# A hybrid attention and recurrence block on one Trainium2 core: the query norms move ahead of the turn, the causal mask moves into a matrix product

## The chip, the core and the metric

One core of a Trainium2 chip runs the whole program: TensorE (PE in the profile; its weight loads are PEld), VectorE (DVE), ScalarE (ACT), GpSimd (POOL), and SyncE (SP), which issues nearly all DMA transfers. Each engine has its own queue of instructions and works through it in order; semaphores hold one engine until another has produced what it reads. PSUM is the memory that TensorE's products add up in, SBUF the other one on the chip. The metric is device time of one execution in microseconds (us), the median of several.

## The reference, cut to what matters

```python
mod = silu(c) @ ada_w + ada_b                    # 2048 x 12288, one vector
h = rms_norm(x, norm_mix_g) * (1 + sc1) + sh1    # x: 256 x 2048
z = h @ w_in                                     # q, kc, vc, ks, vs, kw, vw, gl, xr, xg
q = rope(rms_norm(q, q_norm_g), pos)             # 8 heads of 128
ks = rope(rms_norm(ks, k_norm_g[1]), pos)        # 2 key heads; kw the same
gates = sigmoid(gl + gate_b)
o_attn = nsa_attention(...)   # gates of compressed, selected and window attention
o_rnn = rglru_branch(xr, xg, ...)                # causal conv, gated linear recurrence
x = x + gt1 * (concat(rms_norm(o_attn), rms_norm(o_rnn)) @ w_out)
x = x + gt2 * peer_ffn(rms_norm(x, norm_ffn_g) * (1 + sc2) + sh2, ...)
```

In `nsa_attention` each of three branches is a softmax of scaled scores under a mask. The sequence has 256 tokens, so both the selected branch and the window branch are plain causal attention over all of it, with other keys and values. `rglru_branch` computes `a = exp(-8 r softplus(-lam))` and `b = sqrt(1 - a^2) * i * u` and scans `h = a h + b` over the tokens. The last part, the feed-forward of 16384 experts, takes about three quarters of the time, and the change does not touch it.

## The kernel before

Tokens stand in two tiles of 128 (`tb` 0 and 1). The large products are made in three float32r passes, for which each weight tile (`raw`, 1 MB, by SP's queue) is split by ACT into `wh` (L206) and by DVE into the rest `wl` (L207). The input projection is computed in pieces: `q0` (heads 0 to 3 of q) first, then the key blocks, then the blocks b0 to b3, of which b2 holds heads 4 to 7 of q (`q1`) and b0, b1, b3 the recurrence's inputs. `rest` adds a block's products to `part` tiles on DVE (L544).

`ev_q` takes four heads of q: ACT sums the squares, DVE turns them by the rotary tables into `zr_q` (L610 to L613), PE transposes `zr_q` into the PSUM tile `tp_q` (L623), and ACT copies that to `qT`. Beside it DVE forms the inverse norms in `rsqrt` (L404 to L410: three setup operations and three Newton rounds of three, each dependent on the one before) and puts them, times the softmax scale, into `rq` (L640). Keys are treated otherwise: `ev_kv` multiplies the norms into `zr_k` on ACT (L659) before the transposes.

`scores(sp, g, tb)` handles four heads of key group g and one token tile, for both causal branches at once. For each head PE makes two products into `sc` (L808); DVE multiplies by `rq` (L799, only for `tb` 1, the unmasked half) and by `rq` with the mask added (L800), both from PSUM into the SBUF tile `pt`; DVE takes the maxima of `pt` (L803); ACT takes the exponentials of `pt` in place and their sums (L792). `sc`, `tp_q`, `cps`, `ptt`, `rp` and other small products share one PSUM tag with three buffers. `outputs` divides, weighs by the gates and multiplies by the values (`ptt`, `po`); for the compressed branch it multiplies `cs` by `rq` (L831) and adds a mask (L833). `recurrence(gr)` handles two of the eight channel blocks: convolution `u` on DVE (L748), products `rp` on PE (L753), tanh and exp on ACT, and a chain of DVE operations (L760 to L774) that ends in the scans.

`compress` makes the compressed keys: 64 products `cps` (L698), then a norm. `gate_logits` makes `gl`, from a weight tile of 128x384 that is loaded, split, and multiplied in three passes.

What else runs beside: the modulation vector's product with `ada_w`. Part of it is done on PE (`adp`, L268), part on DVE: an `av` tile of 128x2048 is loaded by SP (L219) and multiplied and summed by one DVE instruction of 2.28 us (L228). `av` has two buffers, and the `part` tiles occupy them; one comes free when the last transposes of `part_391` (`tp_r`) are done, the other only when those of `part_392` are, after `gl`.

The order on every engine is fixed when the program is built. A string names what runs beside what:

```python
PROG = 'q0 b0@.2 e0,k0,k1,p0 b1@.4 e1,b2,e2 s0|s1|r0,c0,b3 c1,g0@.2 e3 o0|o1|r1@.3 r2 s3@.25 s2 l0@.25 o2|o3|r3,l1@.3'
```

`e2` is `ev_q` for q1, `s0` to `s3` are the calls of `scores` (g = n // 2, tb = n % 2), `c1` ends `compress`, `g0` is `gate_logits`, `l0` and `l1` make the second `xg` block. Streams joined by `|` advance in turn, one `yield` each; `@.2` feeds that many `av` products for each `yield`. A scheduler then orders the instructions by readiness and priority. So s0 and s1 (key group 0) form a first score stretch, some 243 to 261 us, and s3 and s2 a second one, some 302 to 324 us. Two recurrences, r0 and r1, run beside or just behind the first, r2 and r3 around the second. Then come the output norms (`nha`, `nta`), the output projection `y` (from 366.75 us), the second norm, and from 476.57 us the query products `wq` of the feed-forward.

Of the kernel before, what the change touches and what calls it, by code (L numbers as in the profile page):

```python
# [7 lines left out]
F32 = mybir.dt.float32  # L8
F32R = mybir.dt.float32r
U32 = mybir.dt.uint32  # L10
I32 = mybir.dt.int32
AF = mybir.ActivationFunctionType
OP = mybir.AluOpType
AX = mybir.AxisListType

P = 128
# [51 lines left out]
def kernel(  # L68
# [512 lines left out]
    kT = zp.tile([P, 2, NG, S], F32, name="kT")  # L581
    vv = zp.tile([P, NT, 2, NG, HD], F32, name="vv")
    gates = zp.tile([P, NT, 24], F32, name="gates")
    rq = zp.tile([P, NT, NH], F32, name="rq")
    kcT = zp.tile([P, 32], F32, name="kcT")
    vc = zp.tile([16, NG, HD], F32, name="vc")

    win = oT.rearrange("p h t -> p (h t)").rearrange("p (a l g n) -> p a l g n", a=2, l=32, g=2)
    ckT = xgT.rearrange("p h t -> p (h t)")[:, 0:4 * S].rearrange("p (a g t) -> p a g t", a=2, g=2)
    V.memset(win[:, :, :, :, NCMP:16], 0.0)  # L590
# [38 lines left out]
    def ev_q(j, pst):  # L629
        tab = table(0)  # L630
        s = tp1.tile([P, NT, 4], F32, tag="ssq", bufs=2, name=f"ssq{j}")
        z = []
        for tb in range(NT):
            z.append(zrow(tp1, f"q{j}{tb}"))
            sumsq(s[:, tb], pst[tb], 4, f"q{j}{tb}")
            rope(z[tb], pst[tb], 4, tab[:, tb, 0], tab[:, tb, 1], f"q{j}{tb}")
            yield
        tp = transpose4(z[0], f"q{j}0")
        r = rsqrt(tp1, s.rearrange("p b h -> p (b h)"), HD, 8, f"q{j}")
        V.tensor_scalar(rq[:, :, 4 * j:4 * j + 4], r.rearrange("p (b h) -> p b h", b=NT), SCALE, None, OP.mult)  # L640
        yield
        A.copy(qT[:, 4 * j:4 * j + 4, tbs[0]], tp.rearrange("p (h t) -> p h t", h=4))
        tp = transpose4(z[1], f"q{j}1")
        yield
        A.copy(qT[:, 4 * j:4 * j + 4, tbs[1]], tp.rearrange("p (h t) -> p h t", h=4))
# [90 lines left out]
    def recurrence(gr):  # L736
        n = RG
        if True:
            u = rn.tile([P, n, S], F32, tag="u", bufs=RNB, name=f"u{gr}")
            ta = rn.tile([P, n, S], F32, tag="ta", bufs=RNB, name=f"ta{gr}")  # L740
            ti = rn.tile([P, n, S], F32, tag="ti", bufs=RNB, name=f"ti{gr}")
            xr = xrT[:, n * gr:n * gr + n]
            for c_ in range(n):
                k = n * gr + c_
                A.activation(u[:, c_], xr[:, c_, 0:S], AF.Identity, scale=sm[:, S_CW + k:S_CW + k + 1],
                             bias=sm[:, S_CB + k:S_CB + k + 1])
                for o in range(1, 4):
                    V.scalar_tensor_tensor(out=u[:, c_], in0=xr[:, c_, o:o + S],  # L748
                                           scalar=sm[:, S_CW + 8 * o + k:S_CW + 8 * o + k + 1], in1=u[:, c_],
                                           op0=OP.mult, op1=OP.add)  # L750
                rp = ps_a(f"rp{gr}{c_}")
                for a in range(2):
                    T.matmul(rp[:, a * S:(a + 1) * S], lw[:, a, k], u[:, c_], start=True, stop=True)  # L753
                A.activation(ta[:, c_], rp[:, 0:S], AF.Tanh, scale=0.5, bias=hb[:, 0, k:k + 1])
                A.activation(ti[:, c_], rp[:, S:2 * S], AF.Tanh, scale=0.5, bias=hb[:, 1, k:k + 1])
                A.activation(xr[:, c_, 0:S], ta[:, c_], AF.Exp, scale=nsp[:, k:k + 1], bias=nsp[:, k:k + 1])
                A.activation(ta[:, c_], ta[:, c_], AF.Tanh, scale=spl[:, k:k + 1], bias=spl[:, k:k + 1])

            d = xr[:, :, 0:S]
            V.tensor_scalar(d, d, 0.5, 0.5, OP.mult, OP.add)  # L760
            V.scalar_tensor_tensor(out=u, in0=ti, scalar=1.0, in1=u, op0=OP.add, op1=OP.mult)
            yield
            V.scalar_tensor_tensor(out=ti, in0=ta, scalar=1.0, in1=d, op0=OP.add, op1=OP.mult)
            A.activation(ta, ta, AF.Sqrt)
            yield
            V.scalar_tensor_tensor(out=d, in0=ti, scalar=2.0, in1=d, op0=OP.subtract, op1=OP.mult)
            V.tensor_scalar(ti, d, -2.0, -1.0, OP.mult, OP.add)
            yield
            V.tensor_tensor(u, u, d, OP.mult)
            yield  # L770
            V.scalar_tensor_tensor(out=u, in0=ta, scalar=-1.0, in1=u, op0=OP.mult, op1=OP.mult)
            yield
            for i in range(n):
                V.tensor_tensor_scan(d[:, i], ti[:, i], u[:, i], 0.0, OP.mult, OP.add)  # L774
            yield
# [4 lines left out]
    def scores(sp, g, tb):  # L780

        n = (tb + 1) * P
        sums = sp.tile([P, 4, 2], F32, tag=f"sums{tb}", bufs=1, name=f"sums{tb}{g}")
        pts = [sp.tile([P, 2, n], F32, tag=f"pt{tb}", bufs=4, name=f"pt{tb}{g}{hh}") for hh in range(4)]
        m2 = sp.tile([P, 4, 2], F32, tag=f"m2{tb}", bufs=1, name=f"m2{tb}{g}")
        held[g, tb] = sums, pts
        scs = {}
        for i in range(6):
            if 0 <= i - 2:
                hh = i - 2  # L790
                for br in range(2):
                    A.activation(pts[hh][:, br], pts[hh][:, br], AF.Exp, bias=m2[:, hh, br:br + 1],  # L792
                                 accum_out=sums[:, hh, br:br + 1])
            if 0 <= i - 1 < 4:
                hh = i - 1
                s3 = scs.pop(hh)[:, 0:2 * n].rearrange("p (b n) -> p b n", b=2)
                r1 = rq[:, tb, 4 * g + hh:4 * g + hh + 1]
                if tb == 1:
                    V.tensor_scalar(pts[hh][:, :, 0:P], s3[:, :, 0:P], r1, None, OP.mult)  # L799
                V.scalar_tensor_tensor(  # L800
                    out=pts[hh][:, :, n - P:n], in0=s3[:, :, n - P:n], scalar=r1,
                    in1=caus.unsqueeze(1).to_broadcast([P, 2, P]), op0=OP.mult, op1=OP.add)
                V.tensor_reduce(m2[:, hh], pts[hh], AX.X, OP.max, negate=True)  # L803
            if i < 4:
                h = 4 * g + i
                scs[i] = ps_a(f"sc{tb}{h}")
                for br in range(2):
                    T.matmul(scs[i][:, br * n:(br + 1) * n], qT[:, h, tbs[tb]], kT[:, br, g, 0:n], start=True, stop=True)  # L808
            yield

    def outputs(sp, g, tb):
# [12 lines left out]
        for hh in range(4):  # L824
# [3 lines left out]
        cm = con[:, C_CMP + 16 * tb:C_CMP + 16 * tb + 16].unsqueeze(1).to_broadcast([P, 4, 16])  # L828
        va = con[:, C_VAL + 16 * tb:C_VAL + 16 * tb + 16].unsqueeze(1).to_broadcast([P, 4, 16])
        mx = sp.tile([P, 4], F32, tag="cmx", bufs=2, name=f"cmx{g}{tb}")  # L830
        V.tensor_tensor(pc, cps[:, 0:64].rearrange("p (h n) -> p h n", h=4),  # L831
                        rq[:, tb, hs].unsqueeze(2).to_broadcast([P, 4, 16]), OP.mult)
        V.tensor_tensor(pc, pc, cm, OP.add)  # L833
        V.tensor_reduce(mx, pc, AX.X, OP.max)
        V.tensor_tensor(pc, pc, mx.unsqueeze(2).to_broadcast([P, 4, 16]), OP.subtract)
        A.activation(pc, pc, AF.Exp)
# [581 lines left out]
```

## Time and profile before

| | |
|---|---|
| median of 3 runs | 2052.03 us (2051.98 to 2058.9) |
| profiled execution | 2056.6 us, span 2054.8 us |
| mean granted clock of TensorE | 0.983 of full |
| PE busy | 1979.6 us, 96% of the span |
| DVE busy | 1451.0 us, 71% |
| ACT busy | 1016.1 us, 49% |

The span runs from the first instruction to the last on the core; the execution's own time is 1.8 us longer. Busy shares are means over stages that differ: the stages that the change touches lie between about 205 and 366 us, and in them the DVE is as busy as PE.

### The profile page before, as it was taken

How to read it: one execution, taken by the hardware profiler on the slowest of the kernel's cores; microseconds unless marked ns; L12 is line 12 of the kernel's file. 1: busy time of each engine (PE TensorE's matmuls, PEld its weight loads, DVE VectorE, ACT ScalarE, POOL GpSimd, SP SyncE). 2: the span in 40 equal slices, each digit the busy share in tenths (PEclk: the TensorE clock that was granted, in tenths of full speed). 3: DMA queues.
4: the chain of work that ended last, by engine and by line, in shares of the span. 5: the costliest groups of instructions: out<-in, count | busy, mean ns of one | idle time of the engine just before them, and what ended most of it. 6: DMA issues, size and time to landing. Idle time of an engine off the chain costs nothing.

```text
span 2054.8 us, 31264 instructions
## 1 busy us (share of the span) xinstructions
PE 1979.6 (96%) x12602; PEld 1751.4 (85%) x12602; DVE 1451.0 (71%) x2149; ACT 1016.1 (49%) x1454; POOL 61.0 (3%) x95
## 2 busy tenths in 40 slices
PE   5999998998999999999999999999999999999998
PEld 4777565788999999998888789899999889999997
DVE  7888999887999666546667766665555555555566
ACT  2544676455446988645444334444444444444442
POOL 0000000000000000001000000000000000000000
PEclk8999998898999999999999999999999999999999
DMA  9898778995455666778767777776555666556663
GB/s 361 333 361 337 273 302 326 343 342 207 165 179 192 227 244 244 253 262 308 256 232 259 270 263 258 256 265 209 197 199 200 214 203 208 202 203 207 198 226 130
DMA packets 75873, 509.12 MB, mean 248 GB/s; under 512 B 8528, under 2 KB 9040, under 8 KB 20176
## 3 DMA queue, kind: packets, MB, share of 16 engines
q1 hardware_dynamic: 63792, 450.50, 60.7%
q0 software_dynamic: 11936, 56.63, 8.2%
q8 instruction: 98, 1.61, 0.3%
q14 instruction: 47, 0.39, 0.1%
HBM read 478.78 MB, written 28.31 MB: 247 GB/s over the span
## 4 chain that ended last, share of the span: by engine, by line
PE 64%; issue 16%; DVE 12%; DMA 4%; ACT 2%; POOL 1%; DVEq 0%; SPq 0%; POOLq 0%; ACTq 0%
PE d L374 8%; PE d L373 8%; PE d L372 8%; PE u L356 7%; PE u L355 7%; PE u L357 7%; DVE wl L207 3%; DVE av L228 3%; DMA raw<-in_ada_w_dram 2%; PE wq L372 2%; PE wq L373 2%; PE wq L374 2%; PE y L357 1%; PE y L355 1%; PE y L356 1%
## 5 line engine op out<-in xcount | busy, mean ns | idle before, releaser
L207 DVE TENSOR_TENSOR wl<-raw,wh 128x1024 fp32r<-128x1024 f32 x649 | 788.9, 1221 | 462.8 <-ACT wh L206 460.0
L206 ACT CAST wh<-raw 128x1024 fp32r<-128x1024 f32 x649 | 679.9, 1050 | 808.7 <-PE u L357 374.2
L372 PE MATMUL d<-xH,wh 128*128 128x256 f32 x2048 | 571.4, 279 | 0.0
L374 PE MATMUL d<-xH,wl 128*128 128x256 f32 x2048 | 568.0, 277 | 0.8 <-DVE wl L207 0.7
L373 PE MATMUL d<-xL,wh 128*128 128x256 f32 x2048 | 567.6, 277 | 0.0
L356 PE MATMUL u<-wl,ah 128*128 128x512 f32 x1024 | 400.0, 391 | 4.2 <-DVE wl L207 4.2
L355 PE MATMUL u<-wh,ah 128*128 128x512 f32 x1024 | 398.9, 390 | 0.0
L357 PE MATMUL u<-wh,al 128*128 128x512 f32 x1024 | 398.6, 389 | 0.0
L374 PEld LDWEIGHTS d<-xH,wl 128*128 128x128 f32 x2048 | 384.9, 188 | 1.3 <-DVE wl L207 1.2
L372 PEld LDWEIGHTS d<-xH,wh 128*128 128x128 f32 x2048 | 385.2, 188 | 0.7
L373 PEld LDWEIGHTS d<-xL,wh 128*128 128x128 f32 x2048 | 384.9, 188 | 0.7
L356 PEld LDWEIGHTS u<-wl,ah 128*128 128x128 f32 x1024 | 192.2, 188 | 46.4 <-DVE wl L207 7.4
L357 PEld LDWEIGHTS u<-wh,al 128*128 128x128 f32 x1024 | 192.4, 188 | 40.2
L355 PEld LDWEIGHTS u<-wh,ah 128*128 128x128 f32 x1024 | 192.2, 188 | 39.7
L228 DVE SCALAR_TENSOR_TENSOR av<-av,cb 128x2048 f32<-128x2048 f32 x64 | 145.8, 2283 | 6.2 <-DMA av<-in_ada_w_dram 6.2
L1185 DVE TENSOR_TENSOR oh<-con,idT 128x1024 f32<-128x1024 f32 x64 | 78.0, 1223 | 58.4 <-PE w L1201 58.4
L1206 ACT ACTIVATE oh<-oh,gT 128x128 f32<-128x128 f32 x256 | 83.1, 396 | 24.9 <-DVE oh L1185 24.9
L372 PE MATMUL wq<-xH,wh 128*128 128x256 f32 x256 | 73.5, 288 | 2.5 <-ACT xH L206 2.5
L373 PE MATMUL wq<-xL,wh 128*128 128x256 f32 x256 | 73.2, 286 | 0.0
L374 PE MATMUL wq<-xH,wl 128*128 128x256 f32 x256 | 73.0, 285 | 0.0
L1262 DVE TENSOR_TENSOR acc<-acc,u 128x512 f32<-128x512 f32 x112 | 71.5, 679 | 0.0
L1201 PE MATMUL w<-oh 128*128 128x128 f32 x512 | 69.8, 276 | 0.2 <-ACT stg L1193 0.2
(359 smaller groups left out, 2007.9 us busy)
## 6 DMA issues: line engine op xcount, KB each, us to landing
raw<-in_down_dram SPq DMA_DIRECT2D x128, 1024.0 KB, 5.2
raw<-in_up_dram SPq DMA_DIRECT2D x128, 1024.0 KB, 5.1
av<-in_ada_w_dram SPq DMA_DIRECT2D x64, 1024.0 KB, 7.0
raw<-in_w_a_dram SPq DMA_DIRECT2D x32, 1024.0 KB, 9.0
raw<-in_ada_p_dram SPq DMA_DIRECT2D x16, 1024.0 KB, 7.1
raw<-in_w_out_dram SPq DMA_DIRECT2D x16, 1024.0 KB, 7.9
raw<-in_wq_dram SPq DMA_DIRECT2D x16, 1024.0 KB, 5.2
wd<-stg POOLq DMA_DIRECT2D x8, 2048.0 KB, 8.0
```

What stands on the lines that cost most here:

```text
L206: A.copy(dst_h, src)
L207: V.tensor_tensor(dst_l, src, dst_h.bitcast(F32), OP.subtract)
L228: V.scalar_tensor_tensor(out=t, in0=t, scalar=1.0, in1=cb, op0=OP.mult, op1=OP.mult, accum_out=m)
L355: T.matmul(o, ah, bh, start=first, stop=False)
L356: T.matmul(o, ah, bl, start=False, stop=False)
L357: T.matmul(o, al, bh, start=False, stop=last)
L372: T.matmul(o, wh[:, kk, ws], bH[:, kc], start=f and i % 2 == 0, stop=False)
L373: T.matmul(o, wh[:, kk, ws], bL[:, kc], start=False, stop=False)
L374: T.matmul(o, wl[:, kk, ws], bH[:, kc], start=False, stop=e and i % 2 == 1)
L1185: V.tensor_tensor(oh, iota.unsqueeze(1).unsqueeze(1).to_broadcast([P, 4, 2, P]), idT[:, 4 * q:4 * q + 4].unsqueeze(3).to_broadcast([P, 4, ...
L1206: A.activation(ohs[p_][:, k, 0], ohs[p_][:, k, 0], AF.Copy, scale=gT[:, t:t + 1])
L1262: V.tensor_tensor(a, a, pst[tb], OP.add)
```

## The change

1. `ev_q` forms the norms first, multiplies them by the scale (L643 of the changed kernel, which takes L640's place), and ACT multiplies them into the turned queries, four heads for each token tile (eight activations of 128x128 for each of q0 and q1). Only then are they transposed. `rq` is gone.
2. `scores` adds the mask by a third product for each head: the identity `idr` times the mask `car`, both float32r, 256 columns (L810 of the changed kernel). DVE takes the maxima directly from `sc` (L811), and ACT's exponentials read `sc` and write `pt`. The loop has five steps, not six, and a `sc` tile is held until its exponentials are done.
3. `recurrence`: the line `d = 0.5 d + 0.5` goes from DVE to ACT as `d + 1`, and three constants behind it are rescaled.
4. `outputs`: the product with `rq` is dropped.
5. Two copies make `idr` and `car`; `vc` moves into a part of `xgT`.

```diff
 def ev_q(j, pst):
...
+        r = rsqrt(tp1, s.rearrange("p b h -> p (b h)"), HD, 8, f"q{j}")
+        V.tensor_scalar(r, r, SCALE, None, OP.mult)
+        yield
+        for tb in range(NT):
+            for h in range(4):
+                hs = slice(h * HD, (h + 1) * HD)
+                A.activation(z[tb][:, hs], z[tb][:, hs], AF.Copy, scale=r[:, 4 * tb + h:4 * tb + h + 1])
+            yield
         tp = transpose4(z[0], f"q{j}0")
-        r = rsqrt(tp1, s.rearrange("p b h -> p (b h)"), HD, 8, f"q{j}")
-        V.tensor_scalar(rq[:, :, 4 * j:4 * j + 4], r.rearrange("p (b h) -> p b h", b=NT), SCALE, None, OP.mult)
...
 def recurrence(gr):
...
-            V.tensor_scalar(d, d, 0.5, 0.5, OP.mult, OP.add)
+            A.activation(d, d, AF.Identity, bias=1.0)
...
 def scores(sp, g, tb):
...
-        for i in range(6):
-            if 0 <= i - 2:
-                hh = i - 2
+        for i in range(5):
+            if i:
+                s3 = scs.pop(i - 1)
                 for br in range(2):
-                    A.activation(pts[hh][:, br], pts[hh][:, br], AF.Exp, bias=m2[:, hh, br:br + 1],
-                                 accum_out=sums[:, hh, br:br + 1])
-            if 0 <= i - 1 < 4:
-                hh = i - 1
-                s3 = scs.pop(hh)[:, 0:2 * n].rearrange("p (b n) -> p b n", b=2)
-                r1 = rq[:, tb, 4 * g + hh:4 * g + hh + 1]
-                if tb == 1:
-                    V.tensor_scalar(pts[hh][:, :, 0:P], s3[:, :, 0:P], r1, None, OP.mult)
-                V.scalar_tensor_tensor(
-                    out=pts[hh][:, :, n - P:n], in0=s3[:, :, n - P:n], scalar=r1,
-                    in1=caus.unsqueeze(1).to_broadcast([P, 2, P]), op0=OP.mult, op1=OP.add)
-                V.tensor_reduce(m2[:, hh], pts[hh], AX.X, OP.max, negate=True)
+                    A.activation(pts[i - 1][:, br], s3[:, br], AF.Exp, bias=m2[:, i - 1, br:br + 1],
+                                 accum_out=sums[:, i - 1, br:br + 1])
             if i < 4:
                 h = 4 * g + i
-                scs[i] = ps_a(f"sc{tb}{h}")
+                s3 = ps_a(f"sc{tb}{h}")[:, 0:2 * n].rearrange("p (b n) -> p b n", b=2)
+                scs[i] = s3
                 for br in range(2):
-                    T.matmul(scs[i][:, br * n:(br + 1) * n], qT[:, h, tbs[tb]], kT[:, br, g, 0:n], start=True, stop=True)
+                    T.matmul(s3[:, br], qT[:, h, tbs[tb]], kT[:, br, g, 0:n], start=br == 0, stop=False)
+                T.matmul(s3[:, :, n - P:n], idr, car.unsqueeze(1).to_broadcast([P, 2, P]), start=False, stop=True)
+                V.tensor_reduce(m2[:, i], s3, AX.X, OP.max, negate=True)
             yield
```

The order moves with it, at three places above all.

On DVE, at the norms of q1 before the first scores, the kernel before has (one row is one instruction; tile names are followed by their build numbers):

```order
L404 TENSOR_SCALAR rsv_q_1790<-ssq_1762 128x8
L207 TENSOR_TENSOR wl<-raw,wh 128x1024
L405 TENSOR_SCALAR rst_q_1792<-rsv_q_1790 128x8
L800 SCALAR_TENSOR_TENSOR pt_1814<-sc_1819,rq,con 128x256
L406 TENSOR_SCALAR rsr_q_1791<-rst_q_1792 128x8
L207 TENSOR_TENSOR wl<-raw,wh 128x1024
L408 SCALAR_TENSOR_TENSOR rst_q_1792<-rsr_q_1791 128x8
L803 TENSOR_REDUCE m_1818<-pt_1814 128x2
L409 TENSOR_TENSOR rst_q_1792<-rst_q_1792,rsv_q_1790 128x8
L799 TENSOR_SCALAR pt_1823<-sc_1828,rq 128x2x128
L410 SCALAR_TENSOR_TENSOR rsr_q_1791<-rst_q_1792,rsr_q_1791 128x8
L800 SCALAR_TENSOR_TENSOR pt_1823<-sc_1828,rq,con 128x2x128
```

The changed kernel has at the same place:

```order
L207 TENSOR_TENSOR wl<-raw,wh 128x1024
L404 TENSOR_SCALAR rsv_q_1795<-ssq_1772 128x8
L207 TENSOR_TENSOR wl<-raw,wh 128x1024
L405 TENSOR_SCALAR rst_q_1797<-rsv_q_1795 128x8
L228 SCALAR_TENSOR_TENSOR av,mod<-av,cb 128x2048
L406 TENSOR_SCALAR rsr_q_1796<-rst_q_1797 128x8
L408 SCALAR_TENSOR_TENSOR rst_q_1797<-rsr_q_1796 128x8
L409 TENSOR_TENSOR rst_q_1797<-rst_q_1797,rsv_q_1795 128x8
L410 SCALAR_TENSOR_TENSOR rsr_q_1796<-rst_q_1797,rsr_q_1796 128x8
```

The steps of the Newton rounds stood between score operations and now stand by themselves behind two `wl` and one `av` (five more of them follow these rows, then L643, two `part` sums, and then the first maxima). A later place on DVE, the norm of the attention output (`nha`), moves the other way: an `av` product now stands inside its Newton rounds, and two `wl` and one `av` instead of one of each stand between the rounds' end and the first `nta`. At the end of `y`, the last `wl` of the stretch now stands ahead of the last `av` and no longer behind it, ahead of `yt`.

On PE, from the last scores to the products `rp` of the fourth recurrence (some 317 to 334 us in the trace of before), the kernel before has:

```order
L808 MATMUL sc_2441<-kT,qT 128x128 x2
L808 MATMUL sc_2448<-kT,qT 128x128 x2
L268 MATMUL adp_1511<-raw,cs 32x512 x5
L818 MATMUL cs_2548<-kcT,qT 128x16 x4
L818 MATMUL cs_2571<-kcT,qT 128x16 x4
L268 MATMUL adp_1511<-raw,cs 32x512 x7
L753 MATMUL rp_2604<-u_2597,lw 128x256 x2
L753 MATMUL rp_2615<-u_2597,lw 128x256 x2
L855 MATMUL ptt_2642<-con,pt_2424 128x128
```

The changed kernel has at the same place:

```order
L268 MATMUL adp_1521<-raw,cs 32x512 x4
L809 MATMUL sc_2458<-kT,qT 128x128 x2
L810 MATMUL sc_2458<-car,idr 128x256
L821 MATMUL cs_2556<-kcT,qT 128x16 x4
L356 MATMUL xg_0_2465<-wl,xH 128x512
L357 MATMUL xg_0_2465<-wh,xL 128x512
L821 MATMUL cs_2578<-kcT,qT 128x16 x4
L356 MATMUL xg_1_2466<-wl,xH 128x512
L357 MATMUL xg_1_2466<-wh,xL 128x512
L355 MATMUL xg_0_2465<-wh,xH 128x512
```

Ahead of its `rp` follow 19 more products of the `xg` block (22 in all behind the first `cs`) and eight of `adp`; the kernel before has seven of `adp` there, and has made those of `xg` earlier, between its scores and `rp` products (ahead of the third recurrence's `rp` it has 39 of them, the changed kernel 17). In the first score stretch PE's order moves too: the changed kernel makes the products of block b3 (24 of them) ahead of q1's transposes, and the eight score tiles then follow with little between them; the kernel before makes most of b3 between its scores.

On SP, around the load of the gate weights, the kernel before has:

```order
L198 DMA raw<-in_cmp_w_dram 128x2048
L219 DMA av<-in_ada_w_dram 128x2048
L198 DMA raw<-in_cmp_w_dram 128x2048
L201 DMA raw<-in_w_gl_dram 128x384
L201 DMA raw<-in_w_in_dram 128x2048
L196 DMA raw<-in_ada_p_dram 128x2048 x3
L201 DMA raw<-in_w_in_dram 128x2048
```

The changed kernel has:

```order
L219 DMA av<-in_ada_w_dram 128x2048
L196 DMA raw<-in_ada_p_dram 128x2048
L198 DMA raw<-in_cmp_w_dram 128x2048 x2
L219 DMA av<-in_ada_w_dram 128x2048 x3
L201 DMA raw<-in_w_gl_dram 128x384
L201 DMA raw<-in_w_in_dram 128x2048
L196 DMA raw<-in_ada_p_dram 128x2048 x3
```

The gate weights' load (128x384) had one `av` load a little ahead of it and now has three in a row directly ahead of it.

## Rows read from the trace of the kernel before

**Rows 1.** The profile page's first section (busy us, share of the span, instructions).
```profile
PE 1979.6 (96%) x12602; PEld 1751.4 (85%) x12602; DVE 1451.0 (71%) x2149; ACT 1016.1 (49%) x1454; POOL 61.0 (3%) x95
```

**Rows 2.** Windows view; busy us of PE, PEld, DVE, ACT, POOL, granted clock, DMA.
```profile
245.00:260.00 15.00, 15.00 (x184) 11.76 (x186) 15.00 (x40) 12.96 (x39) 0.00 (x0) 1.00 0.64 217
...
300.00:325.00 25.00, 23.33 (x126) 15.91 (x124) 24.77 (x54) 18.72 (x51) 0.00 (x0) 0.93 0.79 310
325.00:347.00 22.00, 16.75 (x59) 9.59 (x60) 21.96 (x44) 12.98 (x28) 0.00 (x0) 0.76 0.92 339
```

**Rows 3.** Waits of PE between 205 and 347 us (total, times, longest).
```profile
PE rp L753 <- DVE u L748: 6.5, 1, 6.5
```

**Rows 4.** Timeline of DVE around q1's norms and the score adds (start, duration).
```profile
242.36 0.17 DVE L404 TENSOR_SCALAR rsv_q<-ssq 128x8 f32<-128x8 f32 x1
...
246.73 2.28 DVE L228 SCALAR_TENSOR_TENSOR av<-av,cb 128x2048 f32<-128x2048 f32 x1
...
249.02 0.41 DVE L760 TENSOR_SCALAR xrT<-xrT 128x512 f32<-128x512 f32 x1
...
251.86 0.15 DVE L640 TENSOR_SCALAR rq<-rsr_q 128x8 f32<-128x8 f32 x1
...
257.26 0.47 DVE L800 SCALAR_TENSOR_TENSOR pt<-sc,rq,con 128x256 f32<-128x256 f32 x1
257.66 0.47 DVE L799 TENSOR_SCALAR pt<-sc,rq 128x256 f32<-128x256 f32 x1
258.05 0.41 DVE L803 TENSOR_REDUCE m<-pt 128x2 f32<-128x256 f32 x1
```

**Rows 5.** Timeline of ACT: key scales, first gate tanh, last exponential.
```profile
226.96 1.28 ACT L659 ACTIVATE zr_k<-zr_k,rsr_k 128x128 f32<-128x128 f32 x4
...
245.43 0.47 ACT L754 ACTIVATE ta<-rp,hb 128x256 f32<-128x256 f32 x1 [1.59 <-PE rp L753]
...
260.59 0.49 ACT L792 ACTIVATE pt<-pt,m 128x256 f32<-128x256 f32 x1
```

**Rows 6.** Timeline of PE: scores, compression, gate logits, `xg` products, outputs.
```profile
243.06 1.48 PE L808 MATMUL sc<-kT,qT 128*128 128x128 f32 x8
...
256.66 3.70 PE L698 MATMUL cps<-raw,oT 128*32 128x128 f32 x128
...
269.85 0.28 PE L357 MATMUL gl<-xH,wl 128*24 128x256 f32 x1
...
291.42 1.12 PE L867 MATMUL po<-pT,vc 15*128 15x512 f32 x2
...
298.25 0.40 PE L357 MATMUL xg<-wh,xL 128*128 128x512 f32 x1
298.49 0.39 PE L355 MATMUL xg<-wh,xH 128*128 128x512 f32 x1
...
345.70 1.12 PE L867 MATMUL po<-pT,vc 15*128 15x512 f32 x2
```

**Rows 7.** Timeline of SP's DMA issues, and landing time of the `av` loads.
```profile
249.04 0.33 SPq L219 DMA_DIRECT2D av<-in_ada_w_dram  x1
...
258.64 0.33 SPq L201 DMA_DIRECT2D raw<-in_w_gl_dram  x1
...
av<-in_ada_w_dram SPq DMA_DIRECT2D x8, 1024.0 KB, 5.0
```

**Rows 8.** Timeline of DVE: attention output norm, then the end of `y`.
```profile
358.69 0.17 DVE L406 TENSOR_SCALAR rsr_nha<-rst_nha 128x2 int32<-128x2 int32 x1
358.90 0.16 DVE L408 SCALAR_TENSOR_TENSOR rst_nha<-rsr_nha 128x2 f32<-128x2 f32 x1
...
361.69 2.28 DVE L228 SCALAR_TENSOR_TENSOR av<-av,cb 128x2048 f32<-128x2048 f32 x1
...
363.90 1.67 DVE L899 SCALAR_TENSOR_TENSOR nta<-oT,sm,rb 128x256 f32<-128x256 f32 x4
...
467.19 1.28 DVE L1014 TENSOR_TENSOR yt<-y,gtr 128x512 f32<-128x512 f32 x2
```

More of the change, by code (lines that the diff above doesn't have):

```diff
@@ L583 @@
     gates = zp.tile([P, NT, 24], F32, name="gates")
-    rq = zp.tile([P, NT, NH], F32, name="rq")
+    idr = zp.tile([P, P], F32R, name="idr")
+    car = zp.tile([P, P], F32R, name="car")
+    A.copy(idr, ident)
+    A.copy(car, caus)
     kcT = zp.tile([P, 32], F32, name="kcT")
-    vc = zp.tile([16, NG, HD], F32, name="vc")
+    vc = xgT[0:16, 6].rearrange("p (g d) -> p g d", g=NG)
     win = oT.rearrange("p h t -> p (h t)").rearrange("p (a l g n) -> p a l g n", a=2, l=32, g=2)
@@ L765, in recurrence @@
             yield
-            V.scalar_tensor_tensor(out=d, in0=ti, scalar=2.0, in1=d, op0=OP.subtract, op1=OP.mult)
-            V.tensor_scalar(ti, d, -2.0, -1.0, OP.mult, OP.add)
+            V.scalar_tensor_tensor(out=d, in0=ti, scalar=4.0, in1=d, op0=OP.subtract, op1=OP.mult)
+            V.tensor_scalar(ti, d, -0.5, -1.0, OP.mult, OP.add)
             yield
@@ L770, in recurrence @@
             yield
-            V.scalar_tensor_tensor(out=u, in0=ta, scalar=-1.0, in1=u, op0=OP.mult, op1=OP.mult)
+            V.scalar_tensor_tensor(out=u, in0=ta, scalar=-0.25, in1=u, op0=OP.mult, op1=OP.mult)
             yield
@@ L830, in outputs @@
         mx = sp.tile([P, 4], F32, tag="cmx", bufs=2, name=f"cmx{g}{tb}")
-        V.tensor_tensor(pc, cps[:, 0:64].rearrange("p (h n) -> p h n", h=4),
-                        rq[:, tb, hs].unsqueeze(2).to_broadcast([P, 4, 16]), OP.mult)
-        V.tensor_tensor(pc, pc, cm, OP.add)
+        V.tensor_tensor(pc, cps[:, 0:64].rearrange("p (h n) -> p h n", h=4), cm, OP.add)
         V.tensor_reduce(mx, pc, AX.X, OP.max)
```

## The prediction

> **What bounds the kernel now.** The page's first section comes first: PE is busy for 1979.6 of 2054.8 us [rows 1]. So little is left to win anywhere, and time can only be won where PE stands still. The windows say where, in the part that the change touches. From 245 to 260 us, the first score stretch, PE and DVE are both busy for 15.00 of 15 us: DVE is full, but PE has other products to make and loses nothing. From 300 to 325 us DVE is busy for 24.77 of 25 us and PE for 23.33; from 325 to 347 us DVE for 21.96 of 22 and PE for 16.75, at a granted clock of 0.76 [rows 2]. The waits give that last gap one name: PE stands 6.5 us for `u` of DVE ahead of the fourth recurrence's `rp` [rows 3]. A reader should take from these views that DVE is the engine waited for between 300 and 334 us, that in the first score stretch the two engines run level, and that behind `y`'s start PE is full, so a shift of `y` or of `wq` goes through to the end of the program one for one. I compared the order of DVE's rows behind the start of `wq`: it is the same in both kernels. The answer is therefore how much earlier or later that point comes.
>
> **What the change takes away.** The starts of successive DVE rows give the price of an operation in a full queue better than its duration, because they overlap: L800 at 257.26, L799 at 257.66, L803 at 258.05, so 0.40 us each for L800 and L799 [rows 4]. Sixteen L800 and eight L799 make 24 x 0.40 = 9.6 us. L760 starts at 249.02 with 0.41 us; four of these, and four small products of `outputs` at no more, are 8 x 0.4 = 3.2 us by duration. I take 11.5 us, since the small ones start closer together. Half of it, 5.7 us, lies in each score stretch. The maxima and their number stay.
>
> **What it adds.** Sixteen mask products on PE: 256 columns each. Products of 512 columns in the same float32r passes start 0.24 us apart (298.25 to 298.49) [rows 6]; half of that is 0.12, and the duration of a `gl` product with 256 columns, 0.28 us, is the upper bound. So 1.9 us, at most 4.5, half in each stretch. In the second it lies in PE's 6.5 us of waiting; in the first it lies in the wait that I come to next. ACT gets sixteen scales at 1.28 / 4 = 0.32 us [rows 5], 5.1 us in all, and four activations of 512 elements at some 0.6 to 1.2 us. Eight scales (q0's) lie where ACT has room; q1's eight lie on the path.
>
> Reading the maxima and exponentials from PSUM has no row here for these very forms. The nearest rows are L799 and L800, which read the same PSUM tile at 256 elements in 0.47 us, against 0.41 for L803 from SBUF at as many [rows 4]. So a maximum costs between nothing and 0.06 us more; 16 x 0.06 = 1.0 us is the upper end, and I take half, 0.5 us, of which the half lies in either stretch.
> [...]
>
> **What it moves: the first stretch gets later.** Before, the first score product starts at 243.06 us [rows 6] although q1's norms are only ready at 251.86 [rows 4]: nothing but L799 and L800 needs them. Now the transposes need them, and in PE's order all of q1's transposes stand ahead of every score but the first. The Newton rounds no longer have partners to hide between. By the order, behind L404 (242.36) come one `wl` (1.1 us), one `av` (2.2 us) and eleven dependent small operations. Where such a chain runs alone, its steps start 0.20 us apart (358.69, 358.90) [rows 8], so 2.2 us: 242.4 + 1.1 + 2.2 + 2.2 = 247.9 us. Then four scales (1.3), transposes, four more scales: first scores at about 250, 7 us later than before.
>
> From there ACT sets the pace. From the first gate tanh (245.43) to the last exponential (260.59 + 0.49) it needed 15.7 us [rows 5]; the tanhs now start about 252, which gives 267.7, and with the score tiles held through their exponentials (three PSUM buffers) I put 1 to 2 us on it: 269, 8 us later. The DVE saving of 5.7 us buys nothing here.
>
> Next late is `gl`. Its weights were requested at 258.64 [rows 7] and are now queued behind three `av` loads, each of which waits until DVE has consumed the one before, since the `part` tiles hold the second buffer. A load lands in 5.0 us [rows 7], an `av` product takes 2.2. The third of the products between is placed just ahead of the last maximum, so it ends at about 267 to 268; the next `av` load goes out there and lands at 273, its product ends at about 275, and in DVE's order the `wl` of `gl` stands behind it: 276. The 48 products of `gl` need 48 x 0.12 = 5.8 us, and I allow 2 more where they don't run smoothly, so `gl` ends between 282 and 284, 12 to 14 us later (before, the last began at 269.85 [rows 6]). Some of this is made up by filler of PE behind `gl` that the later kernel has already made, for which I take off 2 us. The first two outputs, before done at 292.5 (291.42 and 1.12) [rows 6], should then be done at about 303: **+10.6 us at this point.**
>
> **What it moves: the second stretch catches up.** Two things give it back. PE makes 22 products of `xg` fewer ahead of the third recurrence's `rp` and makes them in the place where it waited for 6.5 us: 22 x 0.24 = 5.3 us. And DVE, which sets the pace from 300 to 334 us [rows 2], has 5.7 us less to do, less 0.3 for the maxima. 10.6 - 5.3 - 5.4 = -0.1; since the mask products and the ACT queue take something, I put the last output at +0.7, so 347.5 instead of 346.8 (345.70 and 1.12) [rows 6].
>
> **What it moves: the tail.** Now an `av` product (2.2 us) stands inside the Newton rounds of `nha`, and a second `wl` (1.1 us) ahead of `nta`; `nta` started at 363.90 and `y` waits for it [rows 8]. That is +3.3. At `y`'s end a `wl` no longer stands ahead of `yt` (467.19) [rows 8], but the last `av` still does: between 0 and 1.2 us back, I take 1.0.
>
> **Sum:** 0.7 + 3.3 - 1.0 = +3.0 us. On the profiled execution's 2056.6 us this is 2059.6; it lies 4.6 above the median of the runs, 2052.0, so the median should come out at about **2055 us**. Half a percent, 10.3 us, is about what a measurement of this kernel can tell from no change.
>
> **The rivals.**
> (A) The forecast: lost in the first stretch, given back in the second, a few us lost in the tail. 2048 to 2061, by the bounds above (the catch-up off by 4 either way, the tail by 2). Chance 0.58.
> (B) DVE's saving reaches the end. For it: DVE is at 99% from 300 to 347 us, and PE waits for it there. It needs the first stretch to lose nothing, so that norms and loads come in time after all, for example because the `av` rows find their data earlier than I think. The gain is bounded by DVE's 11.5 us, of which the second stretch alone can give 5.4 plus what the clock at 0.76 cost: 2041 to 2047. Chance 0.14.
> (C) The first stretch's loss stays. The place is the load of `gl`'s weights behind the three `av` loads; its price is +10.6, and with the tail +2.3 it is 13, so 2065. It decides itself at the third recurrence's `rp`: if these come later than 308, the DVE chain behind them ends later than 334 and nothing is given back. For it: the `xg` products may just as well be needed between the scores as filler, and the three held PSUM tiles make the second stretch wait for ACT. Against it: ACT was busy for only 18.72 of 25 us there [rows 2]. Chance 0.20.
> (D) All is hidden but the tail cancels: 2050 to 2054. Chance 0.08.
> [...]
>
> **How the numbers follow.** (D) and nearly all of (A) lie within 10.3 us; of (B) half is beyond it, of (C) three quarters. Faster by over half a percent: 0.07 from (B), and 0.05 for an unseen gain: 0.12. Slower: 0.15 from (C), and 0.06 from (A)'s upper tail: 0.21. Same: 0.67. The range runs from the middle of (B) to the middle of (C): 2044 to 2066.
>
> **What would show it.** In the profile after, the first score product at about 250 us, not 243; the first score stretch's last exponential at 267 to 271; SP's issue of the gate weights at about 268, not 258.6, behind an `av` issue; `gl` ending after 280. PE's wait for `u` ahead of the fourth `rp` should shrink from 6.5 us to under 2, and that `rp` end within 2 us of 334. `y` should begin at 369 to 372 (before 366.75). If the first score starts before 246 us, the step on the norms is wrong; if the last output comes after 352 us, the catch-up is; if `y` starts before 366, I have missed a gain.

## The result and the profile after

The changed kernel takes 2065.72 us (median of 4 runs, 2062.48 to 2067.59); beside it the kernel before took 2053.01. The ratio is 1.0054, 95% interval 1.003 to 1.0078: 12.7 us slower by the medians, just over the half percent that I called the limit. The range, 2044 to 2066, held it by 0.3 us, and that is luck: the forecast case (A) ended at 2061, the likeliest value, 2055, was 11 us too low, and the case that came, slower, had 0.21.

The profiled execution takes 2067.59 us, 11.0 more than that of before. The page's first section of the changed kernel:

```profile
PE 1986.9 (96%) x12618; PEld 1756.3 (85%) x12618; DVE 1443.2 (70%) x2117; ACT 1021.8 (49%) x1476; POOL 61.0 (3%) x95
```

DVE is busy for 7.8 us less than in [rows 1], where the forecast had 11.5 less 0.5. The span is 11.0 us longer all the same. The windows show where the saving went (columns as in [rows 2]):

```profile
245.00:260.00 15.00, 13.57 (x61) 10.10 (x61) 8.82 (x21) 7.44 (x27) 0.00 (x0) 0.81 0.77 280
260.00:280.00 20.00, 13.57 (x168) 10.64 (x168) 18.13 (x33) 13.37 (x41) 0.00 (x0) 0.83 0.52 175
300.00:325.00 25.00, 25.00 (x114) 17.97 (x111) 24.68 (x37) 22.41 (x44) 0.00 (x0) 1.00 0.78 294
325.00:347.00 22.00, 21.63 (x119) 13.22 (x118) 20.95 (x54) 18.02 (x48) 0.00 (x0) 1.00 0.81 292
```

From 245 to 260 us DVE, which was busy for 15.00 of 15, is now busy for 8.82, and PE for 13.57 at a granted clock of 0.81. From 260 to 280 PE is busy for 13.57 of 20. The saving came out as idle time, because nothing was ready to run. (The windows are the same stretches of the clock, not of the work: the changed kernel reaches its scores only at 255 us.) The second score stretch is as forecast: PE, busy for 23.33 and 16.75 before, is now busy for 25.00 and 21.63, and the wait of [rows 3] is gone from the list of PE's waits; between 205 and 376 us that list now has these at its head (the first lies behind the last output):

```profile
PE rbta L891 <- DVE rsr_nha L410: 4.8, 1, 4.8
PE sc L809 <- ACT pt L802: 4.3, 3, 3.2
```

Followed through PE's timeline (start and duration in us; in brackets how long PE had stood and for whom):

```profile
222.30 0.33 PE L627 MATMUL tp_q<-con,zr_q 128*128 128x128 f32 x1
...
231.21 0.79 PE L356 MATMUL r<-wl,xH 128*128 128x512 f32 x1 [0.92 <-DVE wl L207]
...
246.05 0.79 PE L356 MATMUL r<-wl,xH 128*128 128x512 f32 x1 [1.76 <-DVE wl L207]
...
255.07 0.39 PE L809 MATMUL sc<-kT,qT 128*128 128x128 f32 x2
...
269.09 2.08 PE L809 MATMUL sc<-kT,qT 128*128 128x256 f32 x4 [3.23 <-ACT pt L802]
...
271.31 5.26 PE L708 MATMUL cps<-raw,oT 128*32 128x128 f32 x128
...
284.84 0.28 PE L357 MATMUL gl<-xH,wl 128*24 128x256 f32 x1
...
306.40 1.12 PE L868 MATMUL po<-pT,xgT 15*128 15x512 f32 x2
...
336.36 1.99 PE L763 MATMUL rp<-u,lw 128*128 128x256 f32 x8
...
351.33 1.12 PE L868 MATMUL po<-pT,xgT 15*128 15x512 f32 x2
...
374.92 0.79 PE L355 MATMUL y<-wh,xH 128*128 128x512 f32 x1 [3.61 <-ACT xH L206]
...
480.25 2.10 PE L1025 MATMUL x1T<-con,x 128*128 128x128 f32 x8 [4.45 <-issue]
...
487.65 0.79 PE L372 MATMUL wq<-xH,wh 128*128 128x256 f32 x2 [2.52 <-ACT xH L206]
```

In the kernel before, the rows that answer to the first and the last of the fence above, and that [rows 6] does not have, are:

```profile
214.45 0.60 PE L623 MATMUL tp_q<-con,zr_q 128*128 128x128 f32 x4
...
476.57 0.79 PE L372 MATMUL wq<-xH,wh 128*128 128x256 f32 x2 [2.52 <-ACT xH L206]
```

The table puts these beside [rows 6]; the last column is how much later the changed kernel is there. An output's end is its last `po` start plus 1.12.

| place | before | after | later by |
|---|---|---|---|
| q0's first transpose | 214.45 | 222.30 | 7.9 |
| first score product | 243.06 | 255.07 | 12.0 |
| compression's products start | 256.66 | 271.31 | 14.7 |
| last product of `gl` starts | 269.85 | 284.84 | 15.0 |
| first two outputs done | 292.5 | 307.5 | 15.0 |
| last output done | 346.8 | 352.5 | 5.6 |
| `y` starts | 366.75 | 374.92 | 8.2 |
| `wq` starts | 476.57 | 487.65 | 11.1 |

From `wq` to the end both spans have 1578.2 us. So the loss of 11 us in these two executions is made of 15.0 lost, 9.4 won back, and 5.5 lost behind the last output. Each of the traces here and below is of one execution. About 1.0 us of the 15.0 is there already ahead of q0's transposes: the first transposes `tp_c` of the compression's input start at 208.69 before and at 209.66 after. How far executions of one order differ is taken up with e4.

DVE's timeline has the norms of q1, the tail, and the end of `y`:

```profile
246.08 0.17 DVE L404 TENSOR_SCALAR rsv_q<-ssq 128x8 f32<-128x8 f32 x1
...
247.37 2.28 DVE L228 SCALAR_TENSOR_TENSOR av<-av,cb 128x2048 f32<-128x2048 f32 x1
...
365.24 2.29 DVE L228 SCALAR_TENSOR_TENSOR av<-av,cb 128x2048 f32<-128x2048 f32 x1
...
373.20 1.67 DVE L900 SCALAR_TENSOR_TENSOR nta<-oT,sm,rb 128x256 f32<-128x256 f32 x4
...
475.97 2.28 DVE L228 SCALAR_TENSOR_TENSOR av<-av,cb 128x2048 f32<-128x2048 f32 x1
...
478.18 0.68 DVE L1015 TENSOR_TENSOR yt<-y,gtr 128x512 f32<-128x512 f32 x1
```

The steps between 249.58 and 251.58 start 0.20 us apart, as forecast, and `av` stands ahead of them; but the chain began at 246.08, not 242.36 [rows 4]. Ahead of the third maximum (260.09) DVE itself stands for 2.25 us until PE has a score for it. In the tail an `av` stands inside the rounds of `nha` (365.24) and `nta` comes at 373.20, 9.3 us later than in [rows 8]. At the end of `y` an `av` starts at 475.97, when PE's last `y` product (475.41) is about done, and `yt` waits behind it until 478.18. SP's timeline has the gate weights:

```profile
253.12 17.65 SPq L219 DMA_DIRECT2D av<-in_ada_w_dram  x3
274.86 0.33 SPq L201 DMA_DIRECT2D raw<-in_w_gl_dram  x1
```

They went out at 274.86, right behind the three `av` loads (one merged row from 253.12 on), 16.2 us later than in [rows 7].

### The profile page after: what moved, and what is told of

It is laid out like the page before. It is cut to its first block, busy times and chain, and to the rows that moved or that the text cites. A ratio compares the mean times of both kernels' runs of the same rounds, so it can differ in the third digit from the quotient of the medians.

```text
span 2065.8 us, 31296 instructions
## 1 busy us (share of the span) xinstructions
PE 1986.9 (96%) x12618; PEld 1756.3 (85%) x12618; DVE 1443.2 (70%) x2117; ACT 1021.8 (49%) x1476; POOL 61.0 (3%) x95
## 4 chain that ended last, share of the span: by engine, by line
PE 65%; issue 16%; DVE 10%; DMA 5%; ACT 2%; POOL 1%; SPq 0%; DVEq 0%; POOLq 0%; ACTq 0%
PE d L374 8%; PE d L372 8%; PE d L373 8%; PE u L356 7%; PE u L355 7%; PE u L357 7%; DVE wl L207 3%; DVE av L228 2%; DMA raw<-in_ada_w_dram 2%; PE wq L372 1%; PE wq L373 1%; PE wq L374 1%; PE y L356 1%; PE y L357 1%; PE y L355 1%
```

## The experiments

Each ran five rounds against the kernel before on the same chip, but for e8 and e9, which had one execution each. Ratios are to the kernel before, with their 95% interval.

**e1: all but the early norms.** From the changed kernel, with `ev_q`, its `rq` and the product of `outputs` as before:

```diff
+                                 scale=rq[:, tb, 4 * g + i - 1:4 * g + i],
...
                 V.tensor_reduce(m2[:, i], s3, AX.X, OP.max, negate=True)
+                V.tensor_scalar(m2[:, i], m2[:, i], rq[:, tb, h:h + 1], None, OP.mult)
```

> Everything of the change but the early norms: the mask comes by a product, maxima and exponentials read the sums in PSUM, ACT takes the recurrence's line; the norms stay beside the transposes and come in as the exponential's scale and as a small factor on the maxima. Theory P (what costs is that the norms now stand ahead of the transposes): first score product back at 242 to 246 us, first outputs done by 296, the time 2043 to 2053, no slower than before. Rival M (the mask products and the score tiles held in PSUM through the exponentials cost it): 2058 to 2066, with PE waiting for ACT's exponentials by 4 us or more as in the changed kernel. Rival L (the late load of the gate weights behind av loads): gl late, 8 us or more behind before, even with the early scores, 2058 or more.

Measured: 2059.89 us, ratio 1.0033 (1.0021 to 1.0045), slower by 6.5 us. First score product at 245.01, first two outputs at 298.3, 5.8 us later than before, last output at 345.4, 1.4 us *earlier*; `wq` at 479.89, 3.3 later. (This profiled execution was the slowest of its runs and lost 7 us more behind `wq`, where the program is the same.) PE waits for `rsr_nha` ahead of `rbta` for 4.8 us, as in the changed kernel, and for the exponentials:

```profile
PE sc L805 <- ACT pt L797: 3.4, 1, 3.4
```

So theory P is not all: without the early norms half the loss remains, though e1 brings work of its own (a factor on the maxima, the product in `outputs` again, and dearer exponentials, see the last section). Rival M has nearly its sign here, a wait of 3.4 us for ACT's exponentials where it named 4; and 4.7 us are lost behind the last output. Rival L named `gl` 8 us or more behind; its last product comes 5.5 us later (275.31).

**e2: the early norms alone.** From the kernel before, with the new `ev_q`, without the product by `rq` in `outputs`, and in `scores`

```diff
-                r1 = rq[:, tb, 4 * g + hh:4 * g + hh + 1]
+                r1 = 1.0
```

> The early norms alone: the query norms are applied by ACT ahead of the transposes, DVE still scales (by one) and adds the mask as before. Theory P: first score product after 252 us, and the whole loss or more, 2062 to 2072, since DVE's saving is missing. Rival M: 2050 to 2056, since no mask product is there and PSUM is freed as before. Rival L: depends on the order of the av loads alone; as late a load of the gate weights as in the changed kernel (after 270 us) goes with 2060 or more.

Measured: 2062.74 us, ratio 1.005 (1.0033 to 1.0066), slower by 9.4 us. First score product at 250.08 (theory P named after 252), first two outputs at 298.6 (6.0 later), last output at 352.6 (5.8 later), `wq` at 488.25 (11.7 later). Nothing is won back in the second stretch here, so what is won back in the changed kernel belongs to the other parts of the change, as forecast. The gate weights' load leaves at 262.81, so rival L has no part in this loss. The tail loses 5.9, with

```profile
PE rbta L893 <- DVE rsr_nha L410: 6.8, 1, 6.8
```

against 2.7 us before. Theory P is right that the early norms cost. The two halves cost 6.0 and 5.8 us at the first outputs, and together 15.0 in the profiled execution of the changed kernel but 9.4 in e4, so nothing is shown of more or less than their sum.

**e3: the recurrence's line alone.** From the kernel before:

```diff
-            V.tensor_scalar(d, d, 0.5, 0.5, OP.mult, OP.add)
+            A.activation(d, d, AF.Identity, bias=1.0)
```

(with the three rescaled constants.)

> Only the recurrence's line from DVE to ACT. All theories: within 3 us of before, 2049 to 2055; DVE has four operations of 0.33 us less, 1.3 us, of which two lie in the stretch from 300 to 334 us where PE waits for DVE.

Measured: 2050.73 us, ratio 0.999 (0.9979 to 1.0): 2.7 us less, at the edge of what can be told from no change. It is harmless, and the only one of these three that does not lose.

**e8 and e9: is it the hold in PSUM?** In the first recurrence the square root, for which ACT loads one table and loads the exponentials' table again behind it (1.28 us each, at 265.00 and 266.94 in the changed kernel), is left out; e8 from the changed kernel, e9 from the one before:

```diff
-            A.activation(ta, ta, AF.Sqrt)
+            A.activation(ta, ta, AF.Copy if gr == 0 else AF.Sqrt)
```

> The changed kernel with the square root of the first recurrence left out (a copy stands in its place), so that ACT loads no table between the exponentials of the first score stretch; PE's order in that stretch is the same. Theory H (the three PSUM tiles of scores are held through the exponentials, so a table load on ACT now stops PE): PE's wait of 3.2 us for ACT's exponentials ahead of the sixth score tile falls under 1 us, and the compression's products start 2.5 to 4 us earlier, at 267 to 269. Rival N (the late start of the scores by the norms is all there is): they start within 1 us of 271.3.

> The kernel before with the same square root left out, as control; its order is otherwise unchanged. Theory H: the score tiles come free when DVE has read them, so the table load stops nothing on PE and the compression's products start within 1 us of 256.7. Rival N: also within 1 us. If they start 2 us or more earlier here too, the table load was on the path already and the hold in PSUM is not what it costs.

Measured: PE's timeline of e8 and, behind it, of e9:

```profile
252.56 0.39 PE L809 MATMUL sc<-kT,qT 128*128 128x128 f32 x2
...
263.75 1.13 PE L809 MATMUL sc<-kT,qT 128*128 128x256 f32 x4 [0.39 <-ACT pt L802]
...
264.93 3.70 PE L708 MATMUL cps<-raw,oT 128*32 128x128 f32 x128
```

```profile
243.37 1.48 PE L808 MATMUL sc<-kT,qT 128*128 128x128 f32 x8
...
256.98 3.26 PE L698 MATMUL cps<-raw,oT 128*32 128x128 f32 x112
```

From the first score product to the compression's products e8 needs 12.4 us where the changed kernel needs 16.2; e9 needs 13.6, as the kernel before does (256.66 - 243.06). PE's wait ahead of the last score tile of the stretch is 0.39 us where it was 3.23. Theory H holds for this stretch: by these two executions the table loads cost the changed kernel 3.9 us on PE, and the kernel before nothing. Of the 3.9, 2.8 are the wait, and 1.0 is the clock behind it: from the last score tile to the compression's products it is 2.22 us there, at a granted clock of 0.50, and 1.18 in e8, where the tile's four products take 1.13 us, as those at 260.92 do in the changed kernel at a clock of 1.00. (The expectation calls that tile the sixth; it is the eighth.) ACT's timeline of the changed kernel shows how:

```profile
265.00 1.28 ACT L774 ACT_TABLE_LOAD   x1
...
266.94 1.28 ACT L802 ACT_TABLE_LOAD   x1
...
268.59 0.36 ACT L802 ACTIVATE pt<-sc,m 128x128 f32<-128x128 f32 x1
```

The two loads stand between exponentials; until the exponentials behind them are done, at 268.95, the fifth score tile holds one of three buffers, which the eighth needs (it starts at 269.09). In the kernel before DVE empties the tiles: PE had begun five of them by 248 us, and the first exponential starts at 248.35.

Two readings need care. The kernel before makes 22 products of b3 and eight `adp` among its scores and never stands, so its 13.6 us cannot be set beside the 12.4 of e8, which makes none of them. Of the runs with the same work in the stretch, e2 is the control: no mask product, tiles emptied by DVE, and the table loads still in ACT's queue. It needs 10.8 us, with 1.9 of waiting at the end for nothing that the profile names:

```profile
250.08 0.39 PE L813 MATMUL sc<-kT,qT 128*128 128x128 f32 x2
...
260.84 3.70 PE L703 MATMUL cps<-raw,oT 128*32 128x128 f32 x128 [1.86 <-issue]
```

So mask products and held tiles together cost 1.6 us in this stretch even without table loads (12.4 against 10.8). And what e8 wins does not reach the end: it took 2064.87 us in its one execution and e9 2049.60, beside 2050.50 for the kernel before. Behind the compression e8's order is another; its last output is done at 344.55, 7.9 us earlier than in the changed kernel, but its `y` starts at 375.51, 0.6 us later.

**e4 to e7: less feed of `av` in the last outputs.** Is the tail's loss only the order of the `av` products? In the string of the order (e4 changed kernel, e5 as e1, e6 before, e7 as e3):

```diff
-PROG = 'q0 b0@.2 e0,k0,k1,p0 b1@.4 e1,b2,e2 s0|s1|r0,c0,b3 c1,g0@.2 e3 o0|o1|r1@.3 r2 s3@.25 s2 l0@.25 o2|o3|r3,l1@.3'
+PROG = 'q0 b0@.2 e0,k0,k1,p0 b1@.4 e1,b2,e2 s0|s1|r0,c0,b3 c1,g0@.2 e3 o0|o1|r1@.3 r2 s3@.25 s2 l0@.25 o2|o3|r3,l1@.1'
```

> The changed kernel with the feed of av products in the stream of the last outputs cut from 0.3 to 0.1 a step: no av then stands between the attention output's norm and the first nta, neither inside the Newton rounds nor behind them, nor as the last thing ahead of yt. Theory T (of the 12.7 us lost, what is lost behind the last output, 5 us from 352 us on, is the order of the av products alone): y starts 5 to 6 us earlier, 369 to 370, and the time is 2057 to 2061. Rival F (the tail is late only because the outputs are late): the time stays within 2 us of the changed kernel's, 2064 to 2067.

> The kernel with the late norms (mask product, PSUM reads, ACT's line, norms as the exponential's scale) with the same cut of the feed. Theory T: its loss of 6.5 us lay behind the last output, which came 1.4 us earlier than before, so it now gains: 2048 to 2053. Rival F: 2058 to 2061, as without the cut.

> The kernel before with the same cut of the feed, as the control: in it one wl and one av stand between the norm and nta, and both go away. Theory T: 2 to 3.4 us off, 2049 to 2052. Rival F: no change, 2052 to 2054. If the cut takes as much here as in the two others, it is a gain for itself and not what the change lost.

> The recurrence's line on ACT (2.7 us faster alone) with the same cut. Theory T: both gains add, 2046 to 2049. Rival F: 2050 to 2052.

Measured: e4 2069.78 (ratio 1.009, 1.0076 to 1.0103), e5 2072.79 (1.0111, 1.0092 to 1.013), e6 2067.55 (1.0082, 1.0065 to 1.0098), e7 2063.25 (1.0055, 1.0043 to 1.0067). All lose, the kernel before 16 us by it. In e4 `y` starts at 367.85, 7.1 us earlier than in the changed kernel, but not for theory T's reason: the last output is 6.6 us earlier too (345.8), and 5.6 of these are there at the first two outputs, where PE's order is still the changed kernel's. From the last output to `y` it is 22.0 us, and 22.5 in the changed kernel. And what was put off is paid behind `y`, where PE has nothing else; of e4's waits of PE from 360 us on:

```profile
PE wq L372 <- ACT xH L206: 10.2, 1, 10.2
```

`wq` cannot start before the modulation of the second norm is complete, and that needs all of these products. Theory T and rival F both fall.

e4 also shows how far two executions of one order differ. Up to the first outputs PE's order is the changed kernel's. PE's timeline, and a row of DVE's:

```profile
229.60 0.50 PE L356 MATMUL r<-wl,xH 128*128 128x512 f32 x1 [0.92 <-DVE wl L207]
...
250.43 0.39 PE L809 MATMUL sc<-kT,qT 128*128 128x128 f32 x2
...
265.64 5.37 PE L708 MATMUL cps<-raw,oT 128*32 128x128 f32 x128
...
300.80 1.12 PE L868 MATMUL po<-pT,xgT 15*128 15x512 f32 x2
```

```profile
241.77 0.17 DVE L404 TENSOR_SCALAR rsv_q<-ssq 128x8 f32<-128x8 f32 x1
```

The first two outputs are done at 301.9, 9.4 us later than before, not 15.0. Of the 5.6 us between, 1.6 are there at `tp_c` (208.04 and 209.66), 3.0 more arise up to the first score product and 1.0 between it and the compression's products. These 4.0 are TensorE's clock. In both executions PE stands 0.92 us ahead of the same product of an input block (229.60 and 231.21); from this product to the start of the fourteenth of the run it is 5.72 us in the changed kernel's execution, with starts 0.43 apart at a granted clock of 0.50 (231.21 to 236.93), and 3.08 in e4, with starts 0.23 apart, as products of this size have them in the changed kernel at a clock of 1.00 (329.61 to 333.96). Another 0.4 us comes the same way in the products behind 246.05 (241.79 in e4), and the 1.0 from the last score tile to the compression's products (1.18 us in e4, 2.22 there).

**e10 to e12: more feed.** The other way, `l1@.5` in the same place (e10 changed kernel, e11 as e1, e12 as e3), and in e11 also

```diff
-    with tc.high_priority(offset=0):
+    with tc.high_priority(offset=100):
         rba = norm_stats(sp, rb2, oT, "a")
```

> The changed kernel with the feed of av products in the last outputs raised from 0.3 to 0.5 a step, the other way than the cut that cost 4 to 14 us: the last av products come earlier and none stands ahead of the last yt. Theory O (the changed kernel owes av products when the outputs end, and what is owed is paid where PE waits, in the norm behind y): the wait of 4.45 us at y's end falls under 3 us and the time is 1 to 4 us below the changed kernel's, 2061 to 2064.5. Rival D (the tail's loss has another cause): within 1 us, 2064.5 to 2067. Rival B (more av products now delay the outputs' own work): slower, 2067 or more.

> The late norms with the feed raised in the same way, and a priority on the attention output's norm so that wl and av no longer stand behind its rounds (one wl does). Theory O: of 6.5 us lost, 4.7 lay behind the last output and come back for the most part: 2052 to 2056. Rival D: 2058 to 2061.

> The recurrence's line on ACT alone (2.7 us faster) with the feed raised to 0.5. Theory O: this kernel owes nothing, so little comes of it, 2048 to 2051; it is the version that I expect to beat both kernels. Rival B: 2052 or more.

Measured: e10 2070.52 (ratio 1.008, 1.006 to 1.0099), e11 2071.53 (1.0085, 1.0066 to 1.0104), e12 2055.76 (1.001, 0.9998 to 1.0021). Of e10's waits of PE from 360 us on (its first outputs, in the same order again, are done at 307.0):

```profile
PE y L355 <- ACT wh L206: 4.2, 2, 2.9
...
PE y L356 <- DVE wl L207: 3.4, 3, 1.8
...
PE x1T L1025 <- issue: 1.5, 1, 1.5
```

The wait at `y`'s end, 4.4 us in the changed kernel, falls to 1.5 as theory O says, and `wq` follows the last `y` product by 9.3 us where it was 12.2. But `y` itself now waits for its weights (4.2 and 3.4 us), and its last product ends 9 us later. Theory O holds for the one wait and fails for the sum; ACT, which splits those weights, stands 3.7 us for the `w_out` loads between 370 and 430 us, where it is 1.2 in the changed kernel. That the earlier `av` loads take their place in SP's queue is read from the order, and not shown by a run. No version beats the kernel before by more than can be told from no change; e3 comes nearest.

## Why the prediction was right, and where it was wrong

**The mechanism held.** Lost in the first stretch, won back in the second, a few us lost in the tail: all three are in the trace, and `gl`'s weights behind the `av` loads, PE's vanished wait and the `av` inside the norm's rounds stand where the prediction put them. The catch-up, sized at 9.9 us, was 9.4. The sign that I had set for a wrong catch-up, a last output after 352 us, came all the same (352.45), since it was set as a time and what it started from was larger. For the same reason the fourth recurrence's `rp` ends at 338.35 (336.36 and 1.99), 2 us outside what I had named.

**The first stretch: 10.6 forecast, 15.0 in the profiled execution.** I had named about 250 us for the first score product, 267 to 271 for the last exponential, about 268 for the gate weights' issue and 303 for the first outputs. The profiled execution has 255.07, 273.08, 274.86 and 307.5; e4 has 250.43, 267.41, 269.00 and 301.9, which is near the forecast, and e10 has 252.91, 269.89, 270.10 and 307.0 (with 1.8 us of it there at `tp_c`, 210.44). So the step "the first stretch gets later" held, and what it lacked is a term for TensorE's clock, which the sum put at nothing without a reason, and a width: the bounds of (A) allow 4 us for the catch-up and 2 for the tail, and none for this stretch. The clock made 4.0 us between the profiled execution and e4. Whether it did so in the runs of the changed kernel that left no trace (2062.48 to 2066.98) stays open.

**Two terms inside it.** The sentence that q0's eight scales lie where ACT has room looked at ACT's time only: q0's norms gate its transposes as well, which start 7.9 us later. But nothing of it is left at q1's norms: they start at 241.77 in e4, and at 242.36 before; the 246.08 of the profiled execution is the clock and the later start of its span. I put 1 to 2 us on the score tiles held in PSUM, in ACT's chain, and there they do not show: from the first gate tanh to the last exponential it is 14.7 us (258.34 to 273.08), and 13.7 in e4, where I had 15.7 and the 1 to 2. On PE they cost more than that: from the first score product to the compression's products e4 and e10 need 15.2 us and e2, with the same work but the mask products, and no held tiles, 10.8; 2.8 of these 4.4 are the table loads. I had ACT's loads in hand, and did not ask what a tile waits behind when ACT, and no longer DVE, sets it free.

**The tail's end had the wrong sign: 1.0 us back was forecast, 2.9 more were lost.** From `y`'s start to `wq` it was 109.8 us before and 112.7 after. The forecast took a `wl` away from ahead of `yt` and left the `av` there. What counts is what DVE has just begun when `y` ends: before, a `wl` of 1.2 us, so that `yt` started at 467.19, 1.3 us behind the start of the last `y` product (465.91); after, the `av` of 2.28 us (475.97), so that it started at 478.18, 2.8 behind (475.41). This makes 1.6 of the 2.9: PE stands 4.45 us ahead of `x1T`, and 2.87 before. In e10, whose last `av` starts at 461.9, that wait is 1.5. The other 1.3 lie inside `y`, where 20 products instead of 12 start 0.43 us apart and not 0.23, the clock again: 0.50 was granted from 374.92 to 380.20 and from 387.30 to 390.30, and before from 366.75 to 372.04. So the sentence that a shift goes through one for one behind `y`'s start did not hold either. Which order would cost nothing was not found and stays open.

The sum: 5.63 instead of 0.7 at the last output, 2.54 instead of 3.3 up to `y`, 2.91 instead of -1.0 behind it: 11.1 instead of 3.0.

**The rivals.** (C)'s mechanism was in part what came: 2065 was its price, though not by its rule: the third recurrence's `rp` came at 309.9, later than the 308 that it named, and the second stretch caught up 9.4 us all the same. (B) is out: no run with a part of the change in it but e3 is faster than the kernel before, and that by 2.7 us at the edge of what can be told. (D) fell with the first stretch.

**What the reads from PSUM cost.** The forms' durations after (busy us, mean ns), then before:

```profile
L811 DVE TENSOR_REDUCE m<-sc 128x2 f32<-128x512 f32 x8 | 5.5, 685 | 1.7 <-PE sc L810 1.7
...
L811 DVE TENSOR_REDUCE m<-sc 128x2 f32<-128x256 f32 x8 | 3.2, 415 | 2.8 <-PE sc L810 2.8
...
L802 ACT ACTIVATE pt<-sc,m 128x256 f32<-128x256 f32 x16 | 7.4, 472 | 2.4 <-DVE m L811 2.4
...
L802 ACT ACTIVATE pt<-sc,m 128x128 f32<-128x128 f32 x16 | 5.7, 374 | 0.1
```

```profile
L803 DVE TENSOR_REDUCE m<-pt 128x2 f32<-128x512 f32 x8 | 5.4, 674 | 0.0
...
L803 DVE TENSOR_REDUCE m<-pt 128x2 f32<-128x256 f32 x8 | 3.2, 409 | 0.0
...
L792 ACT ACTIVATE pt<-pt,m 128x256 f32<-128x256 f32 x16 | 8.0, 498 | 1.6 <-DVE m L803 1.6
L792 ACT ACTIVATE pt<-pt,m 128x128 f32<-128x128 f32 x16 | 6.2, 390 | 3.1 <-DVE m L803 3.1
```

A maximum from PSUM takes 6 to 11 ns more (415 against 409 at 256 elements, 685 against 674 at 512), so I took too much with half of 0.06 us. The exponentials are 16 to 26 ns shorter (374 against 390 at 128 elements, 472 against 498 at 256), and the read of the sum behind each is 21 ns longer (208 against 187), so over the 32 of them 0.4 us is left of it: 19.8 us with their reads, against 20.2.

## What to carry to other kernels

Ask of work taken from a full engine whether another engine waits for it there: where PE had stood 6.5 us for `u`, that wait was gone after the change; taken where that engine ran level with PE, the work came back as idle time (DVE busy for 8.82 of 15 us). When an operation moves ahead of a transpose or a product, follow what stands behind that product in the in-order queue to the next place that others wait for, at every use of the code: at q1 it made the scores late, at q0 nothing was left of it. Before a few us between two profiles are put down to the change, look for another execution of the same order: here 5.6 us of 15.0 were not in it. When a reader of PSUM changes engine, ask what stands in the new engine's queue ahead of the reads, table loads among it (here two of 1.28 us), and how many buffers there are (here three).

## What was not expected of the hardware

The exponential with a scale read from a tile for each partition (e1) takes 473 ns at 128 elements and 565 at 256, against 374 and 472 with no such scale in the changed kernel: about 95 ns for each, 3 us more on ACT over the 32 of them in e1.

After PE had stood for 1.76 us (the row at 246.05), its products of 512 columns started 0.43 us apart until 250.5 and 0.23 from then on: some 4.4 us at a granted clock of 0.50 (246.05 to 250.50; 0.98 from 250.50 to 254.50) behind a wait of under two. Behind the wait of 0.92 us (the row at 231.21) 0.50 was granted for 5.7 us in this execution (231.21 to 236.93); in e4's the starts behind the same wait (229.60) are 0.23 apart.
